# Other start columns for the operands of the feed-forward and memory products in a decoder step

## The chip, the core and the metric

The kernel runs on one core of a Trainium2 chip. The metric is the device time of one execution in microseconds, from its start to its end. Before the change it is 1616.29 us (median of two runs, 1616.22 to 1616.36).

## The reference

One layer of a decoder with three parallel branches is computed for 256 prompt tokens and 8 x 4 sample tokens, 288 in all, in fp32:

```
h = RMSNorm(x);  P = h @ w_in            # columns: conv branch, q/k/v, memory q, three gates
y_A = conv branch, y_B = stick-breaking attention, y_M = attention into 256 memory tokens
x = x + (g_A*y_A + g_B*y_B + g_M*y_M) @ w_o
x = x + relu(RMSNorm(x) @ w_up)^2 @ w_down
```

D_MODEL is 2048 and D_FF is 8192. The memory keys and values of the prompt are computed in the same step: `rms_norm(mem) @ w_mem_kv`. New keys, values and convolution states are outputs too.

## The kernel before

**Tiles.** Tokens lie along the free dimension: an activation is 16 tiles of 128 channels x 288 tokens. Weights come from one array, `wall`, as 504 slabs of 128 x 1024 fp32 in the order in which they are used. A slab holds 8 blocks of 128 x 128. One `main_tile` gives 128 output channels for all 288 tokens from two slabs, 2048 input channels.

**Splitting.** Every product is made from two fp32r halves of each operand: a high half (a cast) and a low half (value less high half). For each slab, ScalarE casts it into a tile of `wh` (L307), and VectorE subtracts into a tile of `wl` (L318). `products` then issues 24 matmuls per slab: for each of the 8 blocks high weights with high activations, high weights with low activations, then low weights with high activations. All pass through the one matmul line L538 (in `chunk`). Weights are the stationary operand, activations the moving one, with 288 columns. In `mem_products` (L591) it is the other way round: the activations of the memory tokens are stationary, and 512 columns of the weights' slab move.

**Where operands start.** The code gives each operand a start column inside its tile:

- weights: `shifted` takes a tile of 1024 + PAD (64) columns and starts at column 0 for the first 16 slabs (memory) and at SHIFT = 5 for all others;
- activations (`Acts`): two tiles of APART = 320 columns; those of 288 tokens start at AHEAD = 4, those of the memory tokens at 32;
- "homes": once attention and convolution are done, `make_homes` takes all tiles of the pools `k4` (1024 columns) and `s` (512 columns) and cuts three pieces and one piece out of them, 320 columns apart, from column HOME = 36. Of the 38 pieces 32 make the 16 homes, pairs of a high and a low half; they hold first the merged branches, then the squared activations of each up part.

The tile lengths 320, 1024, 512 and 1088 are multiples of 64 elements, so a start column has the same place modulo 64 in every tile of a pool.

**Stages.** The order of time is: memory products (16 slabs), convolution, memory query, keys, queries and values of the attention heads, gates and branch outputs, then `out_tile` for the product with w_o (32 slabs), and four passes c of the feed-forward part. A pass has an up part (16 `main_tile` with the normed activations `h2`, from `Acts`, as moving operand; `up_tile` turns the result into a home) and a down part (16 `main_tile` with the 16 homes as moving operand; `down_tile` adds the result to `x1`). A part has 32 slabs and 768 matmuls.

**Order.** A planner (`Order`) merges the jobs into one order on each engine, from costs written into the code (`MM` = 0.13 us a matmul, `dve`, `act`, `pool`) and from flags. It decides when the program is built. A slab's raw tile, and its `wh` and `wl` tiles, have four buffers each; a cast waits until TensorE has read the tile's earlier content.

**Up tile, step by step.** VectorE reads the accumulated product, applies relu and the norm (L1427); GpSimd squares (L1430); ScalarE casts into the home's high half (L1433); VectorE subtracts into the low half (L1435).

Of the kernel before, what the change touches and what calls it, by code (L numbers as in the profile page):

```python
# [8 lines left out]
F32R = mybir.dt.float32r  # L9
# [6 lines left out]
P = 128  # L16
D_MODEL = 2048
KT = D_MODEL // P
# [4 lines left out]
T = NP + NS  # L23
# [14 lines left out]
N_SLABS = 504  # L38
# [37 lines left out]
class Order:  # L76
# [15 lines left out]
    def add(self, gen, rank, at=None):  # L92
        job = Job(gen, rank, self.now.ready if at is None and self.now else at or 0.0)
        self.jobs.append(job)
        was, self.now = self.now, job
        self.step(job)
        self.now = was
# [10 lines left out]
    def give(self, pool, n=1):  # L108
        self.pools[pool] += [self.now.ready] * n
# [45 lines left out]
def dve(n, *flags, **take):  # L155
    return Ask("DVE", 0.155 + n / 950.0, flags, **take)


def act(n, *flags, **take):
    return Ask("ACT", 0.22 + n / 1170.0, flags, **take)  # L160


def pool(n, *flags, **take):
    return Ask("POOL", 0.3 + n / 420.0, flags, **take)


def pe(us, *flags, **take):
    return Ask("PE", us, flags, **take)


def sp(*flags, **take):
    return Ask("SP", 0.45, flags, **take)


APART = 320
AHEAD, HOME = 4, 36
PAD = 64
GRP = 32
SHIFT = 5
MM = 0.13  # L180
MM_MEM = 0.2267

# [2 lines left out]
def tile_decoder_step(ctx: ExitStack, tc: tile.TileContext, xT, memT, wall, cvec, kmat, ptab,  # L185
                      kpool, vpool, mkc, mvc, hist,
                      yT, oK, oV, oCp, oCs, oMK, oMV):
    nc = tc.nc
# [20 lines left out]
    def tl(p, shape, dt=F32):  # L209
        cnt[0] += 1  # L210
        return pools[p].tile(shape, dt, tag=p, name=f"{p}_{cnt[0]}")

    def bank(p):
        return tl(p, [P, 512])
# [24 lines left out]
    first = cm[:, C_BGATE:C_BGATE + 2 * ML].rearrange("p (k t) -> p k t", k=2)  # L239
# [31 lines left out]
    class Slab:  # L271
        def __init__(self, parts):
            self.parts = parts
            self.landed = [Flag() for _ in range(parts)]
            self.split = [Flag() for _ in range(parts)]
# [10 lines left out]
        sl.landed[part].at = order.landed(n * P * 4 / 1e3)  # L286

    def shifted(p, s):
        n = 0 if s < 2 * KT // 2 else SHIFT
        return tl(p, [P, SLAB + PAD], F32R)[:, n:n + SLAB]  # L290

    def due(s):
# [34 lines left out]
    class Acts:  # L327


        def __init__(self, n=T):  # L330
            c = slice(AHEAD, AHEAD + n) if n == T else slice(32, 32 + n)
            self.h, self.l = tl("a", [P, APART], F32R)[:, c], tl("a", [P, APART], F32R)[:, c]
            self.flag = Flag()

# [200 lines left out]

    def chunk(ps, todo, first, last):
        for i, (w, a) in enumerate(todo):
            nc.tensor.matmul(ps, w, a, start=(first and i == 0), stop=(last and i == len(todo) - 1))  # L538

    slab_no = [0]  # L540
    FULL = [k * P for k in range(8)]
# [2 lines left out]
    def products(ps, uses, acts, first=True, last=True, n=T):  # L544

        s = slab_no[0] - 1
        sl = slabs[s]
        high = [(sl.h, c, a, x) for c, a in zip(uses, acts) for x in (0, 1)]
        low = [(sl.l, c, a, 0) for c, a in zip(uses, acts)]
        todo = high + low  # L550
        for i in range(0, len(todo), STEP):
            part = todo[i:i + STEP]
            yield pe(len(part) * MM, *sl.split, *{a.flag for _, _, a, _ in part})
            if i == 0 and first:
                start_slab(s)
            chunk(ps, [(w[:, c:c + P], a.l if x else a.h) for w, c, a, x in part],
                  first and i == 0, last and i + STEP >= len(todo))

    def main_tile(acts, evac, rank=1.0, n_slabs=2):
        yield pe(0.0, pm=1)  # L560
        ps = bank("pm")[:, :T]
        for i in range(n_slabs):
            slab_no[0] += 1
            yield from products(ps, FULL, acts[8 * i:8 * i + 8], i == 0, i == n_slabs - 1)
            give("w")
        add(evac(ps), rank)
# [33 lines left out]
    def conv_products(evacs):  # L600
# [8 lines left out]
        for k2, o in turns:  # L609
# [9 lines left out]
            for i in range(2):  # L619
                todo.append((sl.l, slice(i * 512 + o * P, i * 512 + (o + 1) * P), "h", 2 * k2 + i))  # L620
            yield pe(6 * MM, *sl.split, hx_in[2 * k2], hx_in[2 * k2 + 1])
            if o == 0:
# [698 lines left out]
    homes, homes_in = [], Flag()  # L1321

    class Home:
        def __init__(self, h, l):
            self.h, self.l = h, l

    def make_homes():
        yield sp(*conv_done, *osb_in, k4=bufs["k4"], s=bufs["s"])
        parts = []
        for _ in range(bufs["k4"]):  # L1330
            x = tl("k4", [P, 1024], F32R)
            parts += [x[:, HOME + i * APART:HOME + i * APART + T] for i in range(3)]
        for _ in range(bufs["s"]):
            parts.append(tl("s", [P, 512], F32R)[:, HOME:HOME + T])
        for j in range(KT):
            homes.append(Home(parts[2 * j], parts[2 * j + 1]))
        done(homes_in)


# [12 lines left out]
    merged = [None] * KT  # L1352

    def branch(br, j):
        def evac(ps):
            sig = gates[br, j]
            if br == 2:
                yield dve(T, sig.flag, a=1)
                macc[j] = tl("a", [P, T])
                nc.vector.tensor_mul(macc[j], ps, sig.out)  # L1360
                give("pm")
                give("t")
                return
            yield dve(T, sig.flag)
            nc.vector.tensor_mul(sig.out, ps, sig.out)  # L1365
            give("pm")
            yield dve(T)
            nc.vector.tensor_add(macc[j], macc[j], sig.out)
            give("t")
            if br == 0:  # L1370
                yield act(T, homes_in)
                a = merged[j] = homes[j]
                nc.scalar.copy(a.h, macc[j])
                yield dve(T)
                nc.vector.tensor_sub(a.l, macc[j], a.h.bitcast(F32))
                give("a")
                done(merged_in[j])
        return evac
# [41 lines left out]
        return load, evac  # L1420


    def up_tile(u, f):
        def evac(ps):
            yield dve(T, r2_done, t=1)
            r = tl("t", [P, T])
            nc.vector.scalar_tensor_tensor(r, ps, 0.0, r2, op0=ALU.max, op1=ALU.mult)  # L1427
            give("pm")
            yield pool(T)
            nc.gpsimd.tensor_mul(r, r, r)  # L1430
            yield act(T)
            a = homes[f]
            nc.scalar.copy(a.h, r)  # L1433
            yield dve(T)
            nc.vector.tensor_sub(a.l, r, a.h.bitcast(F32))  # L1435
            give("t")
            u[f].h, u[f].l = a.h, a.l
            done(u[f].flag)
        return evac
# [48 lines left out]
    def warm_up():  # L1488

        yield pe(4.2, pa=1)  # L1490
        junk = bank("pa")
        one = nc.const_aps.tensor(1.0, [P, 512], mybir.dt.bfloat16)
        for n in [512] * 9 + [256]:
            nc.tensor.matmul(junk[:, :n], one[:, :P], one[:, :n], start=True, stop=True)
        give("pa")

    def main():
        yield from warm_up()
        yield from mem_products()
        yield from conv_products([evac_lin(0, "pa"), evac_gat(0, "pa"), evac_lin(1, "pm"), evac_gat(1, "pm")])  # L1500
        for j in range(2, CT):
            yield from main_tile(hx, evac_lin(j, "pm"))
            yield from main_tile(hx, evac_gat(j, "pm"))
        add(samples(), 2.3)
        for h in range(MH):
            yield from main_tile(hx, mem_head(h), 2 + 0.05 * h)
        for h in range(SH):
            yield from main_tile(hx, sb_key(h), 2.2 + 0.05 * h)
            yield from main_tile(hx, sb_query(h), 2.2 + 0.05 * h)
            yield from main_tile(hx, sb_head(h), 2.2 + 0.05 * h)  # L1510
        yield from branch_products(2, [Late(omem, h, om_in[h]) for h in range(MH)])
        give("a", 8)
        yield from branch_products(1, [Late(osb, h, osb_in[h]) for h in range(SH)])
        give("a", 16)
        yield from branch_products(0, [Late(cact, j, cact_flags[j]) for j in range(CT)])
        give("a", 40)
        mg = [Late(merged, j, merged_in[j]) for j in range(KT)]
        for j in range(KT):
            load, evac = out_tile(j)
            add(load(), 2)  # L1520
            yield from main_tile(mg, evac)
        add(after(sums_2, x1_norm), 0.4)
        hh = [Late(h2, j, h2_in[j]) for j in range(KT)]
        for c in range(D_FF // D_MODEL):
            u = [Later() for _ in range(KT)]
            for f in range(KT):
                yield from main_tile(hh, up_tile(u, f))
            for j in range(KT):
                yield from main_tile(u, down_tile(j, c == D_FF // D_MODEL - 1))

# [167 lines left out]
```

## Time and profile before

| | |
|---|---|
| median of two runs | 1616.29 us |
| profiled execution | 1616.26 us |
| its span, first to last instruction | 1614.3 us |
| matmuls in all | 12638 |
| of them on L538 / L591 | 11712 / 192 |
| HBM traffic over the span | 188 GB/s |

The profile is of one execution, recorded by the hardware. PE is TensorE's matmul, PEld its weight load, DVE VectorE, ACT ScalarE, POOL GpSimd, SP SyncE. In a group of instructions, the numbers behind the bar are busy time in us, mean ns of one, and the idle time of the engine before them with what ended it. In the chain of waits in order of time, a row has its start, its length in us and what ran; "x768" is the number of instructions that were merged. Matmuls overlap, so their durations are not their spacing; the spacing is the length of an unbroken piece over its count.

### The profile page before, as it was taken

The numbers are of one execution on the slowest core, as the hardware profiler recorded it, in microseconds if no ns is written. First come the engines' busy times: TensorE is split into PE (matmuls) and PEld (weight loads), VectorE is DVE, ScalarE is ACT, GpSimd is POOL, SyncE is SP. The second block draws the span as 40 slices with busy tenths as digits, with TensorE's granted clock in tenths as the row PEclk, the third lists the DMA queues.
The fourth block names the chain that finished last, engine by engine and source line by source line (L and its number), as shares of the span: only waits on it lengthen the run. The fifth ranks groups of instructions, "written<-read, shape, count | busy, mean of one in ns | idle before, by whom it ended". The sixth has DMA issues, their size and how long they took to land.

```text
span 1614.3 us, 30755 instructions
## 1 busy us (share of the span) xinstructions
PE 1610.0 (100%) x12638; PEld 1592.5 (99%) x12638; DVE 979.7 (61%) x1503; ACT 753.2 (47%) x1078; POOL 140.2 (9%) x106
## 2 busy tenths in 40 slices
PE   9999999999999999999999999999999999999999
PEld 7999999999999999999999999999999999999999
DVE  7999888877776555655555544555445554455443
ACT  8956877754445334444443333333333333333332
POOL 0030000000000000002222100121002210022100
PEclk9999999999999999999999999999999999999999
DMA  9888768886855555466555555555555555555563
GB/s 328 233 194 277 193 217 241 276 282 248 270 166 170 170 170 170 152 197 191 192 172 167 171 168 168 170 169 171 169 170 170 169 171 168 171 166 168 180 193 100
DMA packets 127200, 310.25 MB, mean 192 GB/s; under 512 B 40018, under 2 KB 49618, under 8 KB 127058
## 3 DMA queue, kind: packets, MB, share of 16 engines
q1 hardware_dynamic: 126770, 307.98, 61.5%
q8 instruction: 99, 1.62, 0.4%
q10 hardware_dynamic: 288, 0.29, 0.1%
q14 instruction: 43, 0.35, 0.1%
HBM read 296.99 MB, written 6.32 MB: 188 GB/s over the span
## 4 chain that ended last, share of the span: by engine, by line
PE 99%; DMA 0%; ACT 0%; DVE 0%; issue 0%
PE pm L538 94%; PE pm L591 3%; PE pa L538 1%; PE pl L1090 1%; PE pl L1274 0%; PE pa L917 0%; DMA wr<-in_wall 0%; PE pa L919 0%; PE pa L918 0%; PE pl L1104 0%; PE pa L1214 0%; PE pa L1250 0%; ACT wh L307 0%; DVE a L1444 0%; PE pl L1312 0%; PE pl L1271 0%
## 5 line engine op out<-in xcount | busy, mean ns | idle before, releaser
L307 ACT CAST wh<-wr 128x1024 fp32r<-128x1024 f32 (+1 forms) x520 | 529.5, 1022 | 634.2 <-PE pm L538 562.3
L318 DVE TENSOR_TENSOR wl<-wr,wh 128x1024 fp32r<-128x1024 f32 (+1 forms) x520 | 618.1, 1193 | 192.3 <-ACT wh L307 190.7
L538 PE MATMUL pm<-a,wh 128*128 128x288 f32 x5184 | 733.3, 292 | 0.0
L538 PEld LDWEIGHTS pm<-a,wh 128*128 128x128 f32 x5184 | 695.1, 188 | 0.4 <-issue 0.4
L538 PE MATMUL pm<-a,wl 128*128 128x288 f32 x2592 | 395.5, 292 | 0.0
L538 PEld LDWEIGHTS pm<-a,wl 128*128 128x128 f32 x2592 | 358.1, 188 | 0.2 <-issue 0.2
L538 PE MATMUL pm<-k,wh 128*128 128x288 f32 x2400 | 338.0, 292 | 0.0
L538 PEld LDWEIGHTS pm<-k,wh 128*128 128x128 f32 x2400 | 321.6, 188 | 0.0
L538 PE MATMUL pm<-k,wl 128*128 128x288 f32 x1200 | 181.8, 292 | 0.0
L538 PEld LDWEIGHTS pm<-k,wl 128*128 128x128 f32 x1200 | 165.4, 188 | 0.0
L1430 POOL TENSOR_TENSOR t<-t 128x288 f32<-128x288 f32 x64 | 96.6, 1510 | 599.3 <-DVE t L1427 599.3
L1444 DVE TENSOR_TENSOR a<-a,pm 128x288 f32<-128x288 f32 x64 | 29.1, 454 | 122.7 <-PE pm L538 122.7
L1427 DVE SCALAR_TENSOR_TENSOR t<-pm,rx 128x288 f32<-128x288 f32 x64 | 29.3, 458 | 92.0 <-PE pm L538 92.0
L1433 ACT CAST k<-t 128x288 fp32r<-128x288 f32 x60 | 26.0, 433 | 126.0 <-POOL t L1430 126.0
L1346 DVE TENSOR_TENSOR t<-pm,rx 128x288 f32<-128x288 f32 x48 | 22.0, 458 | 71.0 <-PE pm L538 71.0
L1435 DVE TENSOR_TENSOR k<-t,k 128x288 fp32r<-128x288 f32 x60 | 28.0, 467 | 59.4 <-ACT k L1433 59.4
L770 DVE SCALAR_TENSOR_TENSOR a<-a,cv,a 128x256 f32<-128x256 f32 x120 | 59.4, 495 | 1.1
L1416 POOL TENSOR_TENSOR t<-t,t 128x288 f32<-128x288 f32 x15 | 21.5, 1436 | 397.9 <-ACT t L1413 397.9
L591 PE MATMUL pm<-wh,a 128*128 128x512 f32 x128 | 34.7, 393 | 0.4 <-ACT wh L307 0.4
L538 PE MATMUL pm<-s,wh 128*128 128x288 f32 x160 | 33.8, 292 | 0.0
L591 PEld LDWEIGHTS pm<-wh,a 128*128 128x128 f32 x128 | 24.1, 190 | 6.2 <-ACT wh L307 1.3
L1365 DVE TENSOR_TENSOR t<-pm,t 128x288 f32<-128x288 f32 x32 | 14.6, 456 | 18.7 <-PE pm L538 12.7
(181 smaller groups left out, 724.1 us busy)
## 6 DMA issues: line engine op xcount, KB each, us to landing
wr<-in_wall SPq DMA_DIRECT2D x488, 512.0 KB, 3.7
wr<-in_wall SPq DMA_DIRECT2D x32, 256.0 KB, 5.2
k<-in_kpool SPq DMA_DIRECT2D x32, 256.0 KB, 6.0
k<-in_vpool SPq DMA_DIRECT2D x32, 256.0 KB, 5.9
k<-in_mkc SPq DMA_DIRECT2D x8, 512.0 KB, 9.4
k<-in_mvc SPq DMA_DIRECT2D x8, 512.0 KB, 7.1
t<-in_xT SPq DMA_DIRECT2D x16, 144.0 KB, 3.6
out_yT<-a SPq DMA_DIRECT2D x16, 144.0 KB, 1.9
```

The costliest lines, as they stand in the source:

```text
L307: nc.scalar.copy(sl.h[:, c], sl.raw[:, c])
L318: nc.vector.tensor_sub(sl.l[:, c], sl.raw[:, c], sl.h[:, c].bitcast(F32))
L538: nc.tensor.matmul(ps, w, a, start=(first and i == 0), stop=(last and i == len(todo) - 1))
L591: nc.tensor.matmul(ps[m], y[:, m * P:(m + 1) * P], z[:, w], start=(k == 0 and j < 2), stop=(k == KT - 1 and j in (4, 5)))
L770: nc.vector.scalar_tensor_tensor(c[:, :NP], up[:, k:k + NP], w, c[:, :NP], op0=ALU.mult, op1=ALU.add)
L1346: nc.vector.tensor_mul(g, ps, rx)
L1416: nc.gpsimd.tensor_add(sq_sum[0], sq_sum[0], res[0])
L1427: nc.vector.scalar_tensor_tensor(r, ps, 0.0, r2, op0=ALU.max, op1=ALU.mult)
L1430: nc.gpsimd.tensor_mul(r, r, r)
L1433: nc.scalar.copy(a.h, r)
L1435: nc.vector.tensor_sub(a.l, r, a.h.bitcast(F32))
L1444: nc.vector.tensor_add(x1[j], x1[j], ps)
```

## The change

Only start columns change. The memory products' weights start at column 36 and their activations at 37. The output part keeps its columns (32 + 4 for homes, 5 for weights). In the up parts of passes 0 to 3 the weights start at 4, 6, 13 and 0 (`UP_SHIFT`), with the activations `h2` at 4 as before. In the down parts the homes start at 32 plus 3, 7, 2 and 6 (`DOWN_AT`), and the weights at one more than these: 4, 8, 3 and 7. A home is no longer a fixed slice: `Home` cuts it anew for each pass out of its piece of 320 columns. `apart` and `like` would split the moving columns in two halves with a gap between them; with `DOWN_GAP` all zero they return what they are given.

```diff
-AHEAD, HOME = 4, 36
+AHEAD, HOME = 4, 32
 PAD = 64
 GRP = 32
 SHIFT = 5
+FF0 = N_SLABS - 4 * 4 * KT
+OUT_AT = 4
+DOWN_AT = (3, 7, 2, 6)
+DOWN_GAP = (0, 0, 0, 0)
+UP_SHIFT = (4, 6, 13, 0)
...
     def shifted(p, s):
-        n = 0 if s < 2 * KT // 2 else SHIFT
+        n = 36 if s < 2 * KT // 2 else SHIFT
+        if FF0 - 2 * KT <= s < FF0:
+            n = OUT_AT + 1
+        elif s >= FF0:
+            c, i = divmod(s - FF0, 4 * KT)
+            n = UP_SHIFT[c] if i < 2 * KT else DOWN_AT[c] + 1
         return tl(p, [P, SLAB + PAD], F32R)[:, n:n + SLAB]
...
-            c = slice(AHEAD, AHEAD + n) if n == T else slice(32, 32 + n)
+            c = slice(AHEAD, AHEAD + n) if n == T else slice(37, 37 + n)
...
-            nc.tensor.matmul(ps, w, a, start=(first and i == 0), stop=(last and i == len(todo) - 1))
+            nc.tensor.matmul(like(ps, a), w, a, start=(first and i == 0), stop=(last and i == len(todo) - 1))
...
     class Home:
-        def __init__(self, h, l):
-            self.h, self.l = h, l
+        def __init__(self, j, at, gap=0):
+            self.h, self.l = (apart(x[:, at:at + T], gap) for x in homes[j])
+
+    def apart(x, gap):
+        if not gap:
+            return x
+        return bass.AP(tensor=x.tensor, offset=x.offset, ap=[list(x.ap[0]), [T // 2 + gap, 2], [1, T // 2]])
+
+    def like(x, a):
+        return x if len(a.shape) == 2 else x.rearrange("p (i t) -> p i t", i=2)
...
-            parts += [x[:, HOME + i * APART:HOME + i * APART + T] for i in range(3)]
+            parts += [x[:, HOME + i * APART:HOME + (i + 1) * APART] for i in range(3)]
         for _ in range(bufs["s"]):
-            parts.append(tl("s", [P, 512], F32R)[:, HOME:HOME + T])
+            parts.append(tl("s", [P, 512], F32R)[:, HOME:HOME + APART])
         for j in range(KT):
-            homes.append(Home(parts[2 * j], parts[2 * j + 1]))
+            homes.append(parts[2 * j:2 * j + 2])
...
-                a = merged[j] = homes[j]
+                a = merged[j] = Home(j, OUT_AT)
...
-    def up_tile(u, f):
+    def up_tile(u, f, c):
...
-            a = homes[f]
+            a = Home(f, DOWN_AT[c], DOWN_GAP[c])
+            r = like(r, a.h)
...
-                yield from main_tile(hh, up_tile(u, f))
+                yield from main_tile(hh, up_tile(u, f, c))
```

## The prediction

> **What bounds the kernel now.** I read the page first, then the chain of waits in order of time, then stretches of the feed-forward part with the busy time of each engine.
>
> ```profile
> span 1614.3 us, 30755 instructions
> PE 1610.0 (100%) x12638; PEld 1592.5 (99%) x12638; DVE 979.7 (61%) x1503; ACT 753.2 (47%) x1078; POOL 140.2 (9%) x106
> PE 99%; DMA 0%; ACT 0%; DVE 0%; issue 0%
> ```
>
> TensorE sets the end: 99% of the chain is its own work. So what counts is how long it takes from the start of one matmul to the start of the next. I call this the step. The mean of one matmul in the groups (292 ns) is no step, since matmuls overlap; the chain in order of time has pieces of unbroken matmuls with their counts, and there the length over the count is the step.
>
> ```profile
> 9.96 35.13 PE pm L591 x155
> ...
> 73.25 56.17 PE pm L538 x432
> ...
> 155.52 3.14 PE pm L538 x24
> 158.66 0.12 PE pa L917
> 158.77 0.12 PE pa L918
> 158.89 0.12 PE pa L919
> 159.01 0.12 PE pa L917
> 159.13 0.12 PE pa L918
> 159.25 0.12 PE pa L919
> 159.37 14.06 PE pm L538 x108
> ...
> 446.48 1164.75 PE pm L538 x8958
> 1611.23 0.02 issue
> 1611.25 0.46 DVE a L1444
> ```
>
> The first row is the chain cut to 10 to 45 us, the others are from the whole chain. The main product line (L538, 288 moving columns) has a step of 56.17/432 = 130.0 ns at 73 us, and 1164.75/8958 = 130.0 ns over everything from 446 us to the end: output, up and down parts run with no gap and all at one step. The memory products (L591, 512 columns) have 35.13/155 = 226.7 ns. The six attention products between 158.66 and 159.37 (256 columns) have 0.71/6 = 118.3 ns.
>
> From the code and the built program the three differ in where their operands start. Counted in fp32 elements modulo 16, the main products' moving operand starts at 4 and their weights at 5; the memory products and these attention products have both at 0. From 256 to 512 columns the step grows by 226.7 - 118.3 = 108.4 ns, 0.423 ns a column. At 288 columns, operands at 0 would by that line take 118.3 + 32 x 0.423 = 131.9 ns. The main products take 130.0. So 1.9 ns per matmul is the one effect of the place that this trace lets one see, if it is the place: the lines, the outputs and the neighbours differ too.
>
> One matmul takes 288 columns; 0.423 ns x 288 is 121.9 ns, so of the 130.0 some 8 ns are not column time. A place can in principle take from these 8 or add to them.
>
> ```profile
> 812.30:912.20 99.90, 99.90 (x771) 99.90 (x770) 54.99 (x74) 41.40 (x53) 23.86 (x16) 1.00 0.54 169
> 912.20:1012.00 99.80, 99.80 (x770) 99.80 (x769) 45.59 (x49) 33.89 (x34) 1.51 (x1) 1.00 0.55 170
> ```
>
> These are the first up part and the first down part (columns: length; PE, PEld, DVE, ACT, POOL busy; granted clock; DMA share; GB/s). PE is busy all the time at clock 1.00. DVE is busy for 55.0 and 45.6 of some 100 us, ACT for 41.4 and 33.9, the DMA for 0.54 and 0.55. Nothing else is near its limit there.
>
> **The change, part by part.** It adds and removes no instruction, no DMA and no wait, and the costs in the order planner stay, so the order on each queue stays too. Only start columns move. The sum is therefore counts of matmuls times a change of step. An up part and a down part each have 16 tiles x 2 slabs x 24 matmuls = 768; four of each make 3072 + 3072 = 6144, and one ns on all of them is 6.1 us.
>
> *Output part.* The diff names OUT_AT = 4 with HOME = 32 and weights at 5. That is column 36 and weights at 5 as before: 0 us.
>
> *Memory products.* 192 matmuls go from weights at 0 and activations at 32 to 36 and 37, the main products' relation. At best they take 130.0 + 224 x 0.423 = 224.8 ns instead of 226.7, or 192 x 1.9 = 0.4 us less.
>
> ```profile
> 20.00:30.00 10.00, 10.00 (x46) 8.29 (x45) 1.00 1.00 349
> 30.00:40.00 10.00, 10.00 (x46) 8.29 (x45) 1.00 1.01 350
> ```
>
> In that stretch the DMA share is 1.00 at 350 GB/s, so a faster TensorE may find its next slab not landed. Bounds -0.4 and 0; I take half, -0.2 us.
>
> *Up parts.* The moving operand stays at 4; the weights, at 5 before, go to 4, 6, 13 and 0 in the four passes. The first has distance 0 between moving and weights, as the attention products have; there I take the whole +1.9 ns, 768 x 1.9 = +1.5 us. 13 is 5 plus 8 elements, so if only the place inside 8 elements (32 bytes) decides, nothing changes: 0. For 6 and 0 no row has such a distance (2 and -4); the bounds are -1.9 and +1.9, and since the nearest rows at another distance than the present one are the slower ones, I take half of the upper, +0.95 ns or +0.7 us each. Sum +2.9 us; bounds -4 x 1.5 = -5.8 and +5.8.
>
> *Down parts.* The moving operands go from 4 to 3, 7, 2 and 6, their weights from 5 to 4, 8, 3 and 7: the distance of one element stays, and both shift together. If the distance alone decides, this costs nothing. If the absolute start decides, no row has a moving operand at such a start; bounds again -1.9 and +1.9 ns, -5.8 and +5.8 us. I take +0.95 ns on all, 3072 x 0.95 = +2.9 us, because all four starts are no longer at a multiple of four elements, which all moving operands in the rows above are.
>
> On that last point the Trainium skill has a rule (SBUF — State Buffer, Door 1: The DMA port swizzle): SBUF has lines of 16 bytes, and each access that crosses to a new line pays a penalty. By it a start off a multiple of four elements touches 73 lines instead of 72. With 121.9/72 = 1.7 ns for a line, an estimate, this is 3072 x 1.7 = +5.2 us for the down parts and 0 for the up parts, whose moving operand stays, against my +2.9 and +2.9; the sum would be nearly the same.
>
> *Other engines.* The writers of these operands write to the new places: the cast and the subtraction of the weights, and the two writes of each up tile.
>
> ```profile
> L318 DVE TENSOR_TENSOR wl<-wr,wh 128x1024 fp32r<-128x1024 f32 x64 | 78.3, 1223 | 32.7 <-ACT wh L307 32.7
> L307 ACT CAST wh<-wr 128x1024 fp32r<-128x1024 f32 x65 | 68.2, 1049 | 93.8 <-PE pm L538 90.4 <-issue 3.5
> L1433 ACT CAST k<-t 128x288 fp32r<-128x288 f32 x60 | 26.0, 433 | 126.0 <-POOL t L1430 126.0
> L1435 DVE TENSOR_TENSOR k<-t,k 128x288 fp32r<-128x288 f32 x60 | 28.0, 467 | 59.4 <-ACT k L1433 59.4
> ```
>
> A slab (24 x 130.0 = 3.12 us of TensorE) needs one cast of 1.05 us and one subtraction of 1.22 us (the groups of the stretch 812 to 1012 us). Casts wait 90.4 of the 200 us for a buffer that TensorE frees: they run ahead. I cost them at 0. Without that cover, a 10% slower cast would be 0.1 us x 256 slabs = 27 us, but it first has to use up more than half of each 3.12 us. The two writes of an up tile are needed 16 tiles later, except the last tile's, whose readers come in the next part after 15 other pairs; the gap-free chain shows that they are in time now.
>
> *Sum.* The profiled execution took 1616.26 us (span 1614.3 and 2.0 around it), beside a median of 1616.29. Then 1616.26 - 0.2 + 0 + 2.9 + 2.9 = 1621.9 us, +0.35%.
>
> **The rivals.**
>
> *Nothing moves.* The 1.9 ns come from the number of columns or from the neighbours and not from the place; TensorE's step is 130.0 wherever operands start. For it: eight parts plus the output part, with moving operands from two kinds of tiles, all show 130.0. Against it: they all have the same place modulo 16, so this is no test. Time 1616.3. Beside it stands the Trainium skill (SBUF — State Buffer, Who interferes with whom): TensorE has two independent read ports, one for the moving operand and one for weights, and never waits on anyone. By that rule the distance could not matter, which speaks for this rival, though not on a misaligned start of one operand.
>
> *Faster.* Part of the 8 ns that are not column time comes from the weights' read and the moving read hitting each other at the present distance or place, and some new places avoid that. At -1.9 ns on all eight parts: 1616.26 - 0.2 - 11.7 = 1604.4; on half of them 1610.2. If the 8 ns went entirely, 6144 x 8 = 49 us, 1567. For it: a rest of 8 ns that no other engine explains. Against it: the rows at other places are slower, not faster.
>
> *Slower by much.* The moving operand is handed to the array in pairs or lines of elements, and a start inside such a group makes groups straddle; or weights at the same place as the moving operand hit it on every line. Price, if the 8 ns that are not column time came twice: 768 x 8 = 6.1 us for each part. It decides over the forecast from three parts on (+18 us, 1634.7); four parts, say all the down parts, give 1616.3 + 24.6 = 1640.9, all eight 1665.4. If every pair of the two odd starts (3 and 7) needed two reads, 1536 x 121.9 = 187 us, 1803. For it: no row has an odd moving start. Against it: the weights have an odd start, 5, and run at 130.0; and distance 0 in the attention products costs 1.9 ns, not 8.
>
> **How the numbers follow.** Forecast 0.50 (1617 to 1628), nothing 0.16, faster 0.18 (of which half lies above 1609, 0.02 below 1584), slower by much 0.16 (0.05 up to 1636, 0.09 above 1648.6). The time is the likeliest case's, 1621.9. The range 1609 to 1636 holds 0.50 + 0.16 + 0.09 + 0.05 = 0.80. Its lower end lies between four parts at -1.9 ns (1610.2) and all eight (1604.4); its upper end is all eight at +1.9 ns (1616.3 + 11.7 = 1628) with one part at twice the 8 ns on top (+6.1) and 2 us to spare. Two per cent, 32 us or 5.3 ns on each of the 6144, is about what a measurement can tell from no change: faster by that 0.02, slower 0.09, within 0.89.
>
> **What would show it right or wrong.** In the changed profile the step of each part, its time over 768, is the whole test. Right: the third up part (weights at 13) at 130.0, the first (at 4) near 131.9, the down parts between 130 and 132, output part 130.0, memory products between 224.8 and 226.7, and no idle time of PE in the feed-forward part. Wrong in the direction "distance decides": all down parts at exactly 130.0. Wrong altogether: a part at 140 or more, or below 128; or a wait of PE for the casts (L307, L318), which would mean that the writers are slower at the new places.

## The result and the profile after

The changed kernel takes 1628.7 us (two runs, 1628.11 and 1629.29) against 1616.29 us: a ratio of 1.0078, 95% interval 1.0062 to 1.0094. It is slower by 12.4 us, less than one per cent.

The page of the changed kernel and its chain of waits in order of time; the product line is L548 there (L538 before), the memory line L601 (L591 before).

```profile
span 1626.0 us, 30755 instructions
PE 1622.1 (100%) x12638; PEld 1604.9 (99%) x12638; DVE 980.3 (60%) x1503; ACT 753.0 (46%) x1078; POOL 139.2 (9%) x106
PE 100%; DVE 0%; issue 0%
```

```profile
72.74 56.17 PE pm L548 x432
...
445.97 1176.94 PE pm L548 x8958
1622.91 0.02 issue
```

TensorE is still without a gap. The piece at 73 us, whose starts the change left alone, has its 130.0 ns a matmul. The long piece from 446 us has the same 8958 matmuls as before and 1176.94 us instead of 1164.75: 12.2 us more, and no wait in it. So the whole loss is in the step, the time from one matmul's start to the next.

The stretches of the output part and of the eight feed-forward parts, cut at the first matmul of each (columns: length; PE, PEld, DVE, ACT, POOL busy; clock; DMA share; GB/s). The counts also take in matmuls that reach over an edge; each part has 768.

```profile
711.99:811.82 99.83, 99.83 (x770) 99.83 (x769) 53.96 (x68) 48.08 (x65) 20.14 (x14) 1.00 0.62 193
811.82:914.21 102.39, 102.39 (x771) 102.39 (x769) 54.94 (x74) 41.28 (x53) 23.85 (x16) 1.00 0.54 164
914.21:1014.05 99.84, 99.84 (x771) 99.84 (x769) 45.51 (x49) 33.82 (x34) 1.51 (x1) 1.00 0.56 169
1014.05:1113.89 99.84, 99.84 (x770) 99.84 (x769) 52.04 (x63) 38.61 (x48) 22.78 (x15) 1.00 0.56 169
1113.89:1214.83 100.94, 100.94 (x771) 100.94 (x770) 45.51 (x49) 33.87 (x34) 1.51 (x1) 1.00 0.54 168
1214.83:1315.94 101.11, 101.11 (x770) 101.11 (x769) 52.00 (x63) 38.60 (x48) 22.72 (x15) 1.00 0.53 166
1315.94:1418.34 102.40, 102.40 (x770) 102.40 (x769) 45.58 (x49) 33.93 (x34) 1.52 (x1) 1.00 0.53 166
1418.34:1519.05 100.71, 100.71 (x771) 100.71 (x769) 51.96 (x63) 38.63 (x48) 22.69 (x15) 1.00 0.54 167
1519.05:1622.73 103.68, 103.68 (x770) 103.61 (x768) 41.97 (x46) 29.95 (x30) 1.52 (x1) 1.00 0.48 153
```

Length over 768 is the step. I write a pair of starts as (moving, weights), in elements; the starts of the homes, the moving operands of the down parts, are counted from column 32 of their piece:

| pass | up part: pair, step | down part: pair, step |
|---|---|---|
| 0 | (4, 4): 133.3 ns | (3, 4): 130.0 ns |
| 1 | (4, 6): 130.0 ns | (7, 8): 131.4 ns |
| 2 | (4, 13): 131.7 ns | (2, 3): 133.3 ns |
| 3 | (4, 0): 131.1 ns | (6, 7): 135.0 ns |

Above 130.0 the up parts add 3.3 + 0 + 1.7 + 1.1 = 6.1 ns and the down parts 0 + 1.4 + 3.3 + 5.0 = 9.8 ns; times 768 that is 4.7 and 7.5 us, together 12.2 us. The span grew by 11.7; the half microsecond between lies at the start, where the first product after the memory's came at 49.2 instead of 49.7 us in this execution.

### The profile page after: what moved, and what is told of

Same layout as the page of the kernel before. It is cut to its first block, busy times and chain, and to the rows that moved or that the text cites. A ratio compares the mean times of both kernels' runs of the same rounds, so it can differ in the third digit from the quotient of the medians.

```text
span 1626.0 us, 30755 instructions
## 1 busy us (share of the span) xinstructions
PE 1622.1 (100%) x12638; PEld 1604.9 (99%) x12638; DVE 980.3 (60%) x1503; ACT 753.0 (46%) x1078; POOL 139.2 (9%) x106
## 4 chain that ended last, share of the span: by engine, by line
PE 100%; DVE 0%; issue 0%
PE pm L548 94%; PE pm L601 3%; PE pa L548 1%; PE pl L1100 1%; PE pl L1284 0%; PE pa L927 0%; PE pa L1513 0%; PE pa L928 0%; PE pa L929 0%; PE pl L1114 0%; PE pa L1224 0%; PE pa L1260 0%; DVE a L1463 0%; PE pl L1322 0%; PE pl L1281 0%
## 5 line engine op out<-in xcount | busy, mean ns | idle before, releaser
L548 PE MATMUL pm<-a,wh 128*128 128x288 f32 x5184 | 736.3, 293 | 0.0
L548 PEld LDWEIGHTS pm<-a,wh 128*128 128x128 f32 x5184 | 697.5, 188 | 0.4 <-issue 0.4
L548 PE MATMUL pm<-a,wl 128*128 128x288 f32 x2592 | 397.1, 293 | 0.0
L548 PEld LDWEIGHTS pm<-a,wl 128*128 128x128 f32 x2592 | 358.9, 188 | 0.2 <-issue 0.2
L548 PE MATMUL pm<-k,wh 128*128 128x288 f32 x2400 | 342.6, 294 | 0.0
L548 PEld LDWEIGHTS pm<-k,wh 128*128 128x128 f32 x2400 | 325.7, 188 | 0.0
L548 PE MATMUL pm<-k,wl 128*128 128x288 f32 x1200 | 184.3, 294 | 0.0
L548 PEld LDWEIGHTS pm<-k,wl 128*128 128x128 f32 x1200 | 167.7, 188 | 0.0
L601 PE MATMUL pm<-wh,a 128*128 128x512 f32 x128 | 34.8, 393 | 0.0
L548 PE MATMUL pm<-s,wh 128*128 128x288 f32 x160 | 34.1, 294 | 0.0
L601 PEld LDWEIGHTS pm<-wh,a 128*128 128x128 f32 x128 | 24.2, 190 | 5.5 <-ACT wh L317 0.6
```

Source lines behind the costliest of these rows:

```text
L548: nc.tensor.matmul(like(ps, a), w, a, start=(first and i == 0), stop=(last and i == len(todo) - 1))
L601: nc.tensor.matmul(ps[m], y[:, m * P:(m + 1) * P], z[:, w], start=(k == 0 and j < 2), stop=(k == KT - 1 and j in (4, 5)))
```

## The experiments

All of them are the changed kernel with other starts. In each, `UP_W` and `DOWN_W` give the weights' start of each pass, a tuple in them one start for each of the part's 32 slabs; `H2_AT` is the start of the normed activations, the moving operand of the up parts.

```diff
-            n = UP_SHIFT[c] if i < 2 * KT else DOWN_AT[c] + 1
+            n = UP_W[c] if i < 2 * KT else DOWN_W[c]
+            n = n if isinstance(n, int) else n[i % (2 * KT)]
...
-            a = h2[j] = Acts()
+            a = h2[j] = Acts(at=H2_AT)
```

My first theory was that the pair of starts sets the step (pair theory). The rivals were that one of the two starts alone does, or their distance alone. The distance alone had fallen with the table above: it is one element in all four down parts, which have four steps.

**Weights' starts alone.**

```diff
-DOWN_AT = (3, 7, 2, 6)
+DOWN_AT = (4, 4, 4, 4)
-UP_SHIFT = (4, 6, 13, 0)
+UP_W = (4, 8, 3, 7)
+DOWN_W = (4, 8, 3, 7)
```

> The weights of the down parts start where the change put them (4, 8, 3, 7), but the homes stay at 4; the up parts get the same four starts with their moving operand at 4, so each pair of starts occurs once with either kind of moving tile. Pair theory (the step follows from the starts of moving operand and weights together): 133.3 ns in the first up part and in the first down part, which both have (4, 4), and each up part within 0.1 ns of its down part. Moving start alone: the down parts are back at 130.0 ns each, since 4 was there before. Weights alone: the down parts keep the changed kernel's 130.0, 131.4, 133.3 and 135.0 ns.

The eight parts of this kernel, up and down in turn:

```profile
812.95:915.33 102.38, 102.38 (x770) 102.38 (x769) 54.89 (x74) 41.28 (x53) 23.82 (x16) 1.00 0.53 165
915.33:1017.74 102.41, 102.41 (x771) 102.41 (x769) 45.48 (x49) 33.85 (x34) 1.51 (x1) 1.00 0.54 166
1017.74:1120.14 102.40, 102.40 (x771) 102.40 (x769) 51.97 (x63) 38.55 (x48) 22.78 (x15) 1.00 0.54 164
1120.14:1222.54 102.40, 102.40 (x771) 102.40 (x770) 45.50 (x49) 33.84 (x34) 1.51 (x1) 1.00 0.54 166
1222.54:1322.38 99.84, 99.84 (x771) 99.84 (x770) 51.97 (x63) 38.56 (x48) 22.71 (x15) 1.00 0.55 169
1322.38:1422.21 99.83, 99.83 (x770) 99.83 (x769) 45.53 (x49) 33.90 (x34) 1.52 (x1) 1.00 0.55 170
1422.21:1522.05 99.84, 99.84 (x770) 99.84 (x769) 51.94 (x63) 38.62 (x48) 22.70 (x15) 1.00 0.54 168
1522.05:1621.89 99.84, 99.84 (x770) 99.77 (x768) 41.92 (x46) 29.94 (x30) 1.51 (x1) 1.00 0.52 160
```

133.3 ns for weights at 4 and at 8, 130.0 for 3 and 7, the same in an up part as in the down part behind it. The kind of tile, and what else differs between up and down parts (VectorE is busy for 54.9 us in the first row and for 45.5 in the second), makes no difference in these four pairs. Moving start alone would have 130.0 in all down parts. Weights alone would have the changed kernel's 130.0, 131.4, 133.3 and 135.0 there; measured are 133.3, 133.3, 130.0 and 130.0. Both fall. One run, 1627.2 us.

**Moving starts alone.**

```diff
-UP_SHIFT = (4, 6, 13, 0)
+UP_W = (21, 37, 20, 36)
+DOWN_W = (5, 5, 5, 5)
```

> The homes of the down parts start where the change put them (3, 7, 2, 6), their weights stay at 5. The up parts have their moving operand at 4 and weights at 21, 37, 20 and 36, that is 16 and 32 elements past 5 and past 4. Moving start alone: the down parts keep 130.0, 131.4, 133.3 and 135.0 ns. Pair theory: at least two of these four change by over 0.5 ns. For the up parts: if a place counts modulo 16 elements, 130.0, 130.0, 133.3 and 133.3 ns; if modulo 32, the second and the fourth alone; the moving operands' and the weights' distances modulo 64 have shown no difference before.

The four up parts have 133.3, 133.3, 133.3 and 131.1 ns, the four down parts:

```profile
915.42:1016.54 101.12, 101.12 (x770) 101.12 (x769) 45.56 (x49) 33.91 (x34) 1.51 (x1) 1.00 0.54 167
1118.93:1220.04 101.11, 101.11 (x770) 101.11 (x769) 45.56 (x49) 33.82 (x34) 1.51 (x1) 1.00 0.55 167
1322.42:1424.81 102.39, 102.39 (x770) 102.39 (x769) 45.56 (x49) 33.91 (x34) 1.51 (x1) 1.00 0.54 166
1525.51:1627.90 102.39, 102.39 (x770) 102.32 (x768) 41.98 (x46) 29.94 (x30) 1.51 (x1) 1.00 0.49 155
```

131.7, 131.7, 133.3 and 133.3 ns for (3, 5), (7, 5), (2, 5) and (6, 5), where the changed kernel had 130.0, 131.4, 133.3 and 135.0 with the same moving starts. The first and the last differ by 1.7 ns, the second by 0.2, the third not at all. Two that change by over 0.5 ns are what the pair theory asked for, and the moving start alone is out again. The two starts do not add either: from (4, 5) at 130.0, moving the weights to 4 costs 3.3 ns and moving the activations to 3 costs 1.7, but both together, (3, 4), cost nothing. The up parts go against my periods of 16 and 32 elements for the weights' start alone: (4, 21) and (4, 37) are not at the 130.0 of (4, 5). One run, 1633.2 us.

**Four maps.** The homes start at 0 to 3, 4 to 7, 8 to 11 and 12 to 15 in the down parts of four kernels, and the weights of slab i at i. The normed activations start at 4, 20, 7 and 23. This is the edit of the first map; the others have other values of `DOWN_AT` and `H2_AT`.

```diff
-DOWN_AT = (3, 7, 2, 6)
+DOWN_AT = (0, 1, 2, 3)
-UP_SHIFT = (4, 6, 13, 0)
+EACH = tuple(range(32))
+UP_W = (EACH, EACH[::-1], tuple(range(32, 64)), tuple(5 * i % 32 for i in EACH))
+DOWN_W = (EACH,) * 4
```

> A map: homes at 0, 1, 2 and 3 in the four down parts, and the weights of slab i of each part at i = 0 to 31, so each pair of starts holds for 24 matmuls. Up parts: moving operand at 4, weights of the slabs at 0 to 31, at 31 to 0, at 32 to 63, and at 5i modulo 32. Pair theory: the up parts repeat each other slab by slab when sorted by the weights' start, within 0.5 ns, and show 133.3 at 4, 130.0 at 5 and 6, 131.7 at 13, 131.1 at 0; (2, 3) gives 133.3 and (3, 4) gives 130.0 in the down parts. If what ran just before decides, the sorted lists differ by over 1 ns. Whether any pair goes below 130.0 is open; the theory of hits between the two reads lets some, one of a fixed rest of 10 ns a matmul lets none.

> The same map with homes at 4, 5, 6 and 7, and the normed activations of the up parts at 20 instead of 4 (16 elements further). Pair theory with a place modulo 16: the first down part (homes at 4) repeats the up parts of the map before, slab by slab; with the moving operand at 20 the up parts show at weights' start w what they showed with 4 at w - 16; (7, 8) gives 131.4 and (6, 7) gives 135.0 ns in the down parts.

> The map with homes at 8 to 11 and the normed activations at 7. In the maps so far the mean over all 32 starts of the weights was 132.2, 135.4, 134.1, 132.2, 132.0, 135.4, 133.7 and 130.4 ns for homes at 0 to 7. If the moving operand's place counts modulo 8, homes at 8, 9, 10, 11 repeat 132.2, 135.4, 134.1 and 132.2 within 0.5 ns; the up parts with moving start 7 then lie between 129.3 and 131.5 ns in the mean whatever the order of the weights' starts (starts 0 to 31 in the first), which would make the moving start the larger of the two influences.

> The map with homes at 12 to 15 and the normed activations at 23. Modulo 8 the down parts repeat 132.0, 135.4, 133.7 and 130.4 ns in the mean, the up parts 130.4; modulo 16 the up parts have what homes at 7 had, and homes at 15 need not.

The down parts of the first map and those of the second. Length over 768 is here a mean over all 32 weights' starts:

```profile
913.54:1015.15 101.61, 101.61 (x771) 101.61 (x769) 45.54 (x49) 33.93 (x34) 1.51 (x1) 1.00 0.54 167
1116.31:1220.34 104.03, 104.03 (x771) 104.03 (x769) 45.53 (x49) 33.96 (x34) 1.51 (x1) 1.00 0.53 163
1321.86:1424.86 103.00, 103.00 (x770) 103.00 (x769) 45.53 (x49) 33.95 (x34) 1.52 (x1) 1.00 0.54 165
1526.25:1627.76 101.51, 101.51 (x770) 101.44 (x768) 41.94 (x46) 29.87 (x30) 1.51 (x1) 1.00 0.50 157
```

```profile
913.54:1014.88 101.34, 101.34 (x770) 101.34 (x769) 45.53 (x49) 33.91 (x34) 1.52 (x1) 1.00 0.54 167
1116.39:1220.37 103.98, 103.98 (x770) 103.98 (x769) 45.53 (x49) 33.94 (x34) 1.51 (x1) 1.00 0.52 163
1321.78:1424.50 102.72, 102.72 (x770) 102.72 (x769) 45.53 (x49) 33.91 (x34) 1.51 (x1) 1.00 0.53 164
1526.03:1626.20 100.17, 100.17 (x770) 100.10 (x768) 41.94 (x46) 29.86 (x30) 1.51 (x1) 1.00 0.50 158
```

| moving start | 0 | 1 | 2 | 3 | 4 | 5 | 6 | 7 |
|---|---|---|---|---|---|---|---|---|
| homes there, ns | 132.3 | 135.5 | 134.1 | 132.2 | 132.0 | 135.4 | 133.8 | 130.4 |
| homes 8 further, ns | 132.4 | 135.6 | 134.2 | 132.1 | 132.0 | 135.5 | 133.6 | 130.4 |

In the mean over the weights' starts the moving start counts modulo 8 elements: the second row repeats the first within 0.2 ns. The up parts fit: 131.7 to 132.2 with the moving start 4 and 131.9 to 132.2 with 20, 130.4 to 130.6 with 7 and with 23. In this mean a moving start of 7 is the best, and 1 and 5 are the worst. The step of single slabs (start of the last matmul less start of the sixth, over 18) shows the weights' share. With the moving start 7 the lowest step is 129.3 ns, below anything before, and it comes at weights' starts 1, 4, 7, 10 and 13; with 15 at 6, 9, 12, 15, 18 and 21; with 23 at 14, 17, 20, 23, 26 and 29. So distances (weights less moving) from -9 to 6 in steps of three give 129.3 there.

The distance does count, then, once the moving start is fixed modulo 8. The maps show this for the other starts too: where both starts are 8 higher, the step is the same. Of the 192 slabs of the first two maps' down parts whose weights start at 0 to 23, 185 have the step, within 0.2 ns, of the slab with both starts 8 higher; with the moving start alone 8 higher only 40 of the slabs at weights 8 to 31 agree as well. A shift of both starts by 16 does the same: in ascending order, the moving start 20 shows at weights 16 to 31 what 4 shows at 0 to 15, within 0.2 ns in 14 of 16 slabs.

The first up part of the first map and the first down part of the second both have the moving start 4 and the weights in ascending order:

```profile
812.19:913.54 101.35, 101.35 (x770) 101.35 (x769) 54.93 (x74) 41.33 (x53) 23.88 (x16) 1.00 0.54 166
```

They agree within 0.1 ns in each slab but the first (131.1 and 130.0 ns), although VectorE is busy for 54.9 us in one and for 45.5 in the other, and ScalarE for 41.3 and 33.9. So what the other engines do at the time leaves no mark on these steps. But the maps also show what the pair theory lacks. In another order of the weights' starts some slabs differ:

```
weights' start (moving 4)      6      8      24     27
ascending                    133.3  133.3  130.0  133.3
descending                   133.3  134.1  130.0  130.0
5i modulo 32                 130.0  134.6  132.3  130.0
```

(4, 6) had run at 130.0 ns through a whole part of the changed kernel, (3, 4) too, and in the ascending map they are at 133.3. (4, 3) is further apart: 130.0 ns in two whole parts of the kernel with weights' starts alone, 134.9 to 135.1 in the three orders here. A slab of 24 matmuls may also be too short to settle, so its step need not be that of a whole part. So I added to the theory: a pair can have more than one steady rhythm, and how the stream enters it decides (entry theory).

**Entry.** Two kernels hold (4, 6) in all four up parts, with other weights' starts in the first slab of some. In the first the down parts have homes at 7 and weights at 1, 4, 10 and 8; in the second they are at (4, 5).

```diff
-UP_SHIFT = (4, 6, 13, 0)
+UP_W = (6, lead(4, 6), lead(5, 6), lead(9, 6))    # first kernel; lead(a, b): a, then 31 times b
+UP_W = (lead(1, 6), 6, lead(1, 6), lead(4, 6))    # second kernel
```

> Up parts: moving operand at 4 and weights at 6 in all four, but the first slab of parts 2, 3 and 4 has its weights at 4, 5 and 9. The pair (4, 6) ran at 130.0 ns in the changed kernel and at 133.3 ns in the first map. If a pair has one step, all four parts have the same, within 0.1 ns, after their first slab. If the pair has two steady rhythms and the entry into it decides (entry theory), at least one part runs at 130.0 and at least one at 133.3 ns from its second slab to its last. Down parts: homes at 7, weights at 1, 4, 10 and 8. Pair theory: 129.3, 129.3, 129.3 and 131.4 ns, as in the map and the changed kernel; entry theory: some of them elsewhere, since they are entered from the up parts here.

> Up parts with the pair (4, 6) throughout, but the first slab has its weights at 1 in the first and third, at 6 in the second and at 4 in the fourth; every down part at (4, 5). Entry theory: 130.0 ns in the first and third up part (after weights at 1 the strided map had this pair at 130.0), 133.3 ns in the second and fourth. One step for a pair: the same in all four.

First kernel, the first two up parts and the first down part between them:

```profile
811.90:914.30 102.40, 102.40 (x770) 102.40 (x769) 54.97 (x74) 41.37 (x53) 23.86 (x16) 1.00 0.54 165
914.30:1013.63 99.33, 99.33 (x770) 99.33 (x769) 45.57 (x49) 33.82 (x34) 1.51 (x1) 1.00 0.55 170
1013.63:1116.04 102.41, 102.41 (x770) 102.41 (x769) 52.05 (x63) 38.66 (x48) 22.72 (x15) 1.00 0.54 165
```

All eight up parts of the two kernels ran at 133.3 ns after their first slab, and the down parts hold what the maps and the changed kernel said: 129.3 for weights at 1, 4 and 10, 131.4 for 8. So both forecasts of the entry theory failed, and within each kernel its rival, one step for a pair, came out. The slab just before does not decide by itself: after weights at 1, (4, 6) had 130.0 ns in the map and has 133.3 here. But the changed kernel's second up part is the same pair at 130.0 for 99.84 us, here it is at 133.3 for 102.4 us: one pair, two steps, each kept for 768 matmuls. What chooses between them I could not steer. One run of each kernel, 1625.6 and 1626.2 us.

**The down parts undone.**

```diff
-DOWN_AT = (3, 7, 2, 6)
+DOWN_AT = (4, 4, 4, 4)
+DOWN_W = (5, 5, 5, 5)
```

> The down parts are back at (4, 5), the up parts stay as changed. If the parts add up: up parts at 133.3, 130.0, 131.7 and 131.1 ns, down parts at 130.0, so 768 x 6.1 ns = 4.7 us above the kernel before, 1621.0 us, plus up to 1.3 us in runs in which the memory products take 233.3 instead of 226.7 ns. If entry matters, the down parts after another up part still show 130.0 or 133.3, each lock being worth 2.6 us.

1624.04 us (four runs), ratio to before 1.0049, 1.0032 to 1.0066. The down parts are at 130.0; the up parts at 133.3, 133.3, 131.7 and 131.1. Their second one, (4, 6), is the surprise and the best case for the entry theory: all operands before the first down part start as in the changed kernel, and the one difference ahead of it is that it now follows (4, 5) and not (3, 4).

```profile
1014.64:1117.04 102.40, 102.40 (x770) 102.40 (x769) 52.04 (x63) 38.66 (x48) 22.75 (x15) 1.00 0.54 165
```

102.40 us here and 99.84 in the changed kernel make 2.6 us; 1621.0 + 2.6 = 1623.6, which is the measured time within its spread. So the two halves of the change do not quite add: undoing the down parts saves 7.5 us there and brings 2.6 back in an up part whose own starts are the same. Chance from run to run is not the likely reason: the four runs here lie within 1.2 us of each other, and so do the two of the changed kernel, less than the 2.6 us by which a switch would move a run. By which of its properties the part before decides, no run shows.

**The memory products alone.** Output, up and down parts at (4, 5), memory at 36 and 37.

> Of the change only the memory products' new starts (36 and 37); output, up and down parts at (4, 5). All parts at 130.0 ns. Pair theory with one step for a pair: 1616.0 us, no difference. Entry theory: the memory products take 226.7 ns in some runs and 233.3 ns in others, as the profiles of the earlier runs show, so the runs spread over 1.3 us, between 1616 and 1617.5 us, where the kernel before spreads over 0.6 us.

Eleven runs between 1615.81 and 1617.44 us, median 1616.95, against a median of 1615.92 for the kernel before (fourteen runs between 1615.58 and 1616.50; a fifteenth, of 4146.77, is left out); the ratio of 1.0005, 0.9996 to 1.0014, can't be told from 1. The memory products' step is seen in the chain cut to 12 to 45 us, of the changed kernel and of the kernel with weights' starts alone, which have the same memory code:

```profile
11.95 33.09 PE pm L601 x146
```

```profile
11.96 33.13 PE pm L604 x142
```

33.09/146 = 226.7 ns and 33.13/142 = 233.3 ns: again one pair and two steps. Three of the eleven profiles with memory at 36 and 37 show 233.3, the others 226.7. On 192 matmuls that is 1.3 us. That it makes the wider spread of these runs fits, but the single runs have no profile, so it is argued, not shown.

**All at 7.** The best place of the maps for every main product, first with the memory products as before, then with theirs at 39 and 39.

```diff
-AHEAD, HOME = 4, 32
+AHEAD, HOME = 7, 32
...
-SHIFT = 5
+SHIFT = 7
...
-OUT_AT = 4
-DOWN_AT = (3, 7, 2, 6)
+OUT_AT = 7
+H2_AT = 7
+DOWN_AT = (7, 7, 7, 7)
...
-UP_SHIFT = (4, 6, 13, 0)
+UP_W = (7, 7, 7, 7)
+DOWN_W = (7, 7, 7, 7)
...
-        n = 36 if s < 2 * KT // 2 else SHIFT
+        n = 0 if s < 2 * KT // 2 else SHIFT    # 39 in the second
...
-            n = OUT_AT + 1
+            n = 7
...
-            c = slice(AHEAD, AHEAD + n) if n == T else slice(37, 37 + n)
+            c = slice(at, at + n) if n == T else slice(32, 32 + n)    # 39 in the second
```

> Every main product (11712 matmuls) with the moving operand at 7 and the weights at 7; the memory products as before (activations at 32, weights at 0). In the maps (7, 7) took 129.3 ns in three of three orders of the weights' starts below 32, with the neighbours 1, 4, 10 and 13 at the same. If that holds outside the map, 11712 x (130.0 - 129.33) = 7.8 us less than before: 1608.2 us. If the entry decides here too, single stages lock at 130.0 or 133.3 and the time lies between 1608 and 1650.

> As the one before, and the memory products' weights and activations both at 39. If the place counts modulo 8 with the distance, the memory products come below 226.7 ns, by up to 192 x 2 ns = 0.4 us; if they have two rhythms there too, single runs differ by 192 x 6.7 = 1.3 us.

The long piece of the chain of the first of them, and its first up and first down part:

```profile
444.40 1158.78 PE pm L551 x8958
```

```profile
808.39:907.72 99.33, 99.33 (x771) 99.33 (x769) 54.95 (x74) 41.22 (x53) 23.87 (x16) 1.00 0.54 170
907.72:1007.05 99.33, 99.33 (x771) 99.33 (x770) 45.55 (x49) 33.83 (x34) 1.51 (x1) 1.00 0.55 171
```

1607.91 us (five runs), ratio to the kernel before 0.9951, 0.9937 to 0.9965: half a per cent faster than the kernel before, clear of the spread of the runs. From 444 us on, output and feed-forward parts included, everything runs at some 129.3 ns (1158.78/8958 = 129.4), and 11712 x 0.67 = 7.8 us stands against a measured gain of 8.0. With the memory products moved too it is 1608.47 us (five runs). Their step is 228.9 ns there (33.19/145), between the two seen before, so moving them to (39, 39) brings nothing:

```profile
11.98 33.19 PE pm L604 x145
```

## Why the prediction was right or wrong

*What bounds the kernel* was right, and so was the form of the sum: counts of matmuls times a change of step, no wait anywhere, casts and subtractions at their old durations hidden.

*The output part* at 0 was right: 99.8 us before and after.

*The memory products* at -0.2 us were wrong. I took the 1.9 ns between their line and the main products' 130.0 as the mark of a worse place. At the main products' place they have 226.7 or 233.3: no gain, or 1.3 us of loss.

*The up parts* were forecast at +2.9 us and took 4.7. For the first part I had read +1.9 ns off the attention products; the place with distance 0 cost 3.3. For the third, 13 instead of 5, I assumed that only the place inside 8 elements counts; it cost 1.7 ns. By the maps 8 elements change nothing only where both starts move by them, and here the distance went from 1 to 9. The fourth cost 1.1 ns where I had 0.95. The second cost nothing where I had half of the bound, and the undone kernel shows that this 0 was one of two rhythms: it could have been 3.3 ns.

*The down parts* were forecast at +2.9 us and took 7.5. This is the term that was mis-sized, and the step behind it is the bound: I let 1.9 ns, the one difference that the trace showed, stand for the most that a place can do. (2, 3) came to 3.3 and (6, 7) to 5.0, and homes at 1 and 5 lie some 5.5 above 130.0 in the mean. The bound came from two other kinds of product and rested on a line through two points. One of them, the attention's 118.3, is the mean of one group of six. All groups of six in the trace before have means of 118.2 to 119.8, so that this point alone is uncertain by most of the 1.9. The reason that I gave for the sign, starts that are no multiple of four, did not hold either: 3 and 7 are no dearer than 0 and 4 in the mean of the maps, and (3, 4) cost nothing in the changed kernel.

Together the two terms were 5.8 us and came to 12.2, so 1621.9 was on the right side and 7 us short; 1628.7 lies in the range and just above the likeliest case's own end of 1628. That is in part luck. Three of the eight parts went past the bound of 1.9 ns (3.3, 3.3 and 5.0), and the sum stayed inside because two others cost nothing, one of them only in the rhythm that it happened to take. Of the signs that I had named, the output part at 130.0 and TensorE without a gap came true. The third up part at 130.0 and the first near 131.9 did not, and of the down parts only two of four lay between 130 and 132.

*The rule of lines* (the Trainium skill, SBUF — State Buffer, Door 1: The DMA port swizzle) would have every start off a multiple of four elements dearer by one line, the same for all four down parts. They differ by up to 5 ns, and in the maps 3 (132.2) costs what 0 and 4 do (132.3, 132.0) while 7 (130.4) is better than either. So a count of lines does not describe the step here. *The rule of two independent read ports* (the Trainium skill, SBUF — State Buffer, Who interferes with whom), read as I read it, would leave the weights' start without any effect while the moving start stays; 133.3 against 130.0 in the kernel with weights' starts alone is against that reading. Whether the ports themselves meet is not shown by that.

*Nothing moves* is out. *Slower by much*, as it was told, is out too: it asked for 8 ns more in a part, and the most is 5.0; the odd starts 3 and 7 are not the dear ones. *Faster* had a true core: there are places below 130.0, though none among the change's eight.

So the cause is shown as far as the two starts go: the step follows the moving start modulo 8, the distance, and what ran before. What stays open is the mechanism inside TensorE: why the moving start counts modulo 8 elements, why a distance in threes is good at 7, and what makes the stream fall into 130.0 or 133.3. An experiment without the weights' reads was not tried, since each matmul carries its load.

## What to carry to other kernels

When TensorE is busy without a gap, look at the step and not at the busy share: here 0.8% and -0.5% hung on nothing but start columns, with the other engines' busy times alike. A bound from the one difference that a trace happens to show is no bound; where a sweep is cheap (a start for each slab of 24 matmuls, in one run), make it before trusting a place. Try a place on the whole stage afterwards, since a pair can settle in more than one rhythm.

## What the runs showed of the hardware

- The step of an fp32r matmul of 288 columns depends on where both operands start in their rows: 129.3 to 140 ns in the slabs of the maps.
- In the mean over weights' starts the moving start counts modulo 8 elements, from 130.4 ns at 7 to 135.5 at 1 and 5.
- With both starts 8 elements higher the step is the same within 0.2 ns in 185 of 192 slabs; with the weights' start alone 16 or 32 higher it is not, 133.3 instead of 130.0 ns for (4, 21) and (4, 37).
- A pair can have two steady steps, (4, 6) 130.0 and 133.3 ns, each kept over 768 matmuls; the 512-column products have 226.7 and 233.3.
- Writing to these places costs ScalarE and VectorE nothing that shows: in the first two parts the casts took 1049 ns before and 1046 after, the subtractions 1223 and 1221.
